# A two-layer hybrid encoder trunk: ScalarE's order in the first phase, and six modulation pieces of each mixer loaded into idle activation slots

## The chip, the core and the metric

The kernel runs on one core of one Trainium2 chip. A core has a matrix engine (TensorE, PE in the profile; its weight loads are listed apart as PEld), a vector engine (VectorE, DVE), an activation engine (ScalarE, ACT), a general engine (GpSimd, POOL) and a sequencer that here issues all data transfers (SyncE, SP). Each engine works through its own list of instructions in order and waits on semaphores for the others. Sixteen DMA engines move data between the chip's memory (HBM) and the core's memory (SBUF); matrix products land in a small accumulator memory (PSUM).

The metric is device microseconds of one execution. The time before is the median of three runs.

## The reference

One input of 256 tokens by 1024 channels goes through two layers. Each layer is a mixer and a squared-ReLU MLP, each with a norm ahead of it and behind it, and each modulated by shift, scale and gate vectors that come from a conditioning vector `c`:

```python
def hybrid_layer(x, c, ada_w, ada_b, ...):
    mod = jax.nn.silu(c) @ ada_w + ada_b
    sh_m, sc_m, gt_m, sh_f, sc_f, gt_f = [t[:, None, :] for t in jnp.split(mod, 6, axis=-1)]
    h = rms_norm(x, g_pre_mix) * (1.0 + sc_m) + sh_m
    proj = h @ w_in                      # rq rk rv rg lx ly fq fk fv ff gates
    ...                                  # retention, RG-LRU recurrence, forgetting attention
    merged = g[:, :, 0] * (y_ret @ ret_w_o) + g[:, :, 1] * (y_lru @ lru_w_o) + g[:, :, 2] * (y_fox @ fox_w_o)
    x = x + gt_m * rms_norm(merged @ w_out, g_post_mix)
    h = rms_norm(x, g_pre_mlp) * (1.0 + sc_f) + sh_f
    f = jnp.square(jax.nn.relu(h @ w1)) @ w2
    return x + gt_f * rms_norm(f, g_post_mlp)
```

`mod` has 6 x 1024 values a layer; its weights `ada_w` are 1024 x 6144 float32 a layer. All weights are float32 and each is read once.

## The kernel before, in words

**Products.** Every float32 operand is split into a rounded part (`hi`) and the remainder (`lo`), and a product is three matmuls, hi by hi, hi by lo and lo by hi (`mm3`, lines 368 to 371). A weight piece of 1024 x 256 is 1 MB; it arrives as two transfers of 512 KB (`raw_half`, line 216) into a ring of five half buffers (`wraw`, `NRAW = 5`). ScalarE writes `hi` (line 240), VectorE writes `lo` (line 241) into one of four half-piece slots `wpair`, or into a slot named in `SLOTS`. The VectorE subtraction is the last reader of the ring buffer. One piece feeds one gemm of 48 matmuls with 256 columns. `prefetch` (line 309) keeps two or three pieces split ahead of the gemm that runs.

**Modulation.** `silu(c) @ ada_w` isn't done on TensorE: a piece of 256 columns, transposed, also comes as two halves into the same ring, and VectorE multiplies each half with the broadcast row `sir` and sums along the row (`ada_sum`, line 301; `ada_step`, line 303). These pieces are woven between the gemm pieces by `weight_order` (line 94): all of them are numbered in one list `ORDER`, and `pos` walks through it. `MIXR` says between which gemms of a mixer the pieces stand, counted from the mixer's end. Mixer 0 has 53 gemms and 12 pieces (`gt_m`, `sc_f`, `sh_f`, four each) behind its gemms 31 to 43; mixer 1 has 61 gemms and 8 pieces (`sc_f`, `sh_f`) behind its gemms 41 to 51. The last 28 gemms of both mixers are the same: fq0, w_l0 to w_l3, fv0 to fv3, fq1 to fq3, fk0 to fk3, g2 0 to 3, w_f 0 to 3, w_o 0 to 3. Counted from the first of them (gemm 25 in mixer 0, 33 in mixer 1) they are called place 0 to 27 below; the pieces stand at places 6 to 18 in mixer 0 and 8 to 18 in mixer 1.

**First phase** (`first_rows`, line 462). The first pieces come by rows of the contraction, so that work starts early: for each k of 0 to 7 a row piece of `sc_m` and `sh_m` weights (two halves) and a row piece of rv and rq/rk weights (two halves). x is turned and scaled by matmuls with a diagonal (`turned`, line 475) into four PSUM tiles of two k each; the first is read in place, the others are copied by ScalarE into `xr` (lines 534 to 536). For each k: VectorE sums the two modulation halves (`row_sums`), ScalarE makes the shift and the scale from them (`sums`, lines 507 and 508), then h (`hh`, line 531, and its exact twin `hf`, line 532); VectorE writes `hl` (line 538); the two weight halves are split; TensorE runs 12 matmuls of 512 columns for rv and 24 of 256 columns for rq and rk (`rvp`, `qkp`). `qkp` needs the four PSUM tiles that held the turned x.

**Order.** A scheduler lays the instructions of each engine in a list at build time, by estimated ready times, with the program's order as the priority. `tc.keep_in_program_order` pins one instruction behind the one traced just before it on its engine.

**Activation slots.** `T1` to `T10` are large SBUF slots, reused in turn by tag (`U`, line 432). In a mixer `T5` holds the retention output until the `rg` gemms are through, `T6` the recurrent branch's `u` until the gelu gate of `ly3` (line 929), `T7` and `T8` its two helpers until the recurrence is through. From fk0 (place 12) on `T5` and `T6` hold the keys and `T7` and `T8` the attention's output. `prefetch` reaches two gemms ahead.

Of the kernel before, what the change touches and what calls it, by code (L numbers as in the profile page):

```python
# [16 lines left out]
KH = 4  # L17
# [16 lines left out]
P = 128  # L34
# [35 lines left out]
def mix_order(l):  # L70
    first = 'g0 g0 g0 g0 lx lx g1 lx g1 lx lru' if l == 0 else \
            'rv rv rv rv rq rk g0 rq rk g0 lx g0 lx g0 lx g1 lx lru g1'
    rest = 'rg rg rg rg g1 w_r w_r w_r w_r g1 ly ly ly ly fq w_l w_l w_l w_l fv fv fv fv fq fq fq fk fk fk fk ' \
           'g2 g2 g2 g2 w_f w_f w_f w_f w_o w_o w_o w_o'
    order = first.split() + rest.split()
    return [(n, order[:i].count(n)) for i, n in enumerate(order)]
# [10 lines left out]
    return name in ('rv', 'w_o', 'w2') or (name == 'w1' and cix < 4)  # L87


MIXR = ((22, 8), (20, 8))  # L90
MLPR = ((5, 28), (5, 15))


def weight_order():
    order = [(n, 0, k) for k in range(KD) for n in ('ada_row', 'row')]

    def spread(l, gem, ada, lo, hi):
        at = [lo + (hi - lo) * i // max(len(ada), 1) for i in range(len(ada))]
        for i, (n, c) in enumerate(gem):
            order.append(('gemm', l, n, c))  # L100
            while at and at[0] <= i:
                at.pop(0)
                order.append(ada.pop(0))
        assert not ada

    for l in range(L):
        n = len(mix_order(l))
        parts = [(l, p) for p in ('gt_m', 'sc_f', 'sh_f')][l:]
        spread(l, mix_order(l), [('ada',) + p + (c,) for p in parts for c in range(4)], *(n - i for i in MIXR[l]))
        parts = [(l, 'gt_f')] + [(i, p) for i in range(l + 1, L) for p in ('sc_m', 'sh_m', 'gt_m')]  # L110
        spread(l, mlp_order(), [('ada',) + p + (c,) for p in parts for c in range(4)], *MLPR[l])
    return order
# [6 lines left out]
def trunk_kernel(ctx, tc, x, c, vec, con, ffw, wts, out):  # L119
# [91 lines left out]
    def raw_half(i, extra=None):  # L211
        n = C if extra is None else C + NH_F
        t = wp.tile([P, KH, n], F32, name="wraw", tag="wraw", bufs=NRAW)
        src = wts[pos[0], i]
        if extra is None:
            nc.sync.dma_start(t.rearrange("p k c -> p (k c)"), src)
        else:
            nc.sync.dma_start(t[:, :, :C], src.rearrange("p (k c) -> p k c", k=KH))
            nc.sync.dma_start(t[:, :, C:], extra[:, i * KH:(i + 1) * KH, :])
        return t  # L220
# [25 lines left out]
    def load_split(l, name, cix):  # L246
        with ExitStack() as stack:
            if (name, cix) in LATE:
                for i in behind.pop(l, ()):
                    stack.enter_context(tc.issue_after(i))  # L250
            return split_of(l, name, cix)
# [44 lines left out]
    def mod_bias(l, o, n, src):  # L296
        V.tensor_tensor(mods[l][:, o:o + n], src, vc(l, 'ada_b')[:, o:o + n], ALU.add)

    def ada_sum(t, m):
        t = t.rearrange("p k c -> p (k c)")  # L300
        V.scalar_tensor_tensor(t, t, 0.5, sir, ALU.mult, ALU.mult, accum_out=m)  # L301

    def ada_step(l, part, cix):
        m = sp.tile([P, 2], F32, name="mcol")
        for j in range(2):
            ada_sum(raw_half(j), m[:, j:j + 1])
        pos[0] += 1
        mod_bias(l, PARTS[part] * 8 + 2 * cix, 2, m)

    ahead = []  # L310

    def prefetch(n=2):
        while len(ahead) < n and pos[0] < len(ORDER):
            o = ORDER[pos[0]]
            if o[0] == 'gemm':
                ahead.append((o[1:], load_split(*o[1:])))
            else:
                ada_step(*o[1:])

# [140 lines left out]
    def first_rows():  # L460
# [13 lines left out]
        def turned(k0):  # L474

            pt = pa.tile([P, 2, 2, P], F32, name="xT", tag="a")
            for k in range(2):
                for t in range(2):
                    T.matmul(pt[:, k, t, :], xs[:, t, (k0 + k) * P:(k0 + k + 1) * P], diag[:, t, :],
                             start=k == t == 0, stop=k == t == 1, skip_group_check=True)  # L480
            return pt.rearrange("p k t c -> p k (t c)")
# [23 lines left out]
        def sums(k, m):  # L505
            kc, o = slice(k, k + 1), 8 * PARTS['sh_m'] + k
            A.activation(a[:, kc], m[:, 0:1], AF.Identity, bias=one[:, kc], scale=vc(0, 'pre_mix')[:, kc])
            A.activation(sh[:, kc], m[:, 1:2], AF.Identity, bias=vc(0, 'ada_b')[:, o:o + 1])

        def halves(k, j, copy=A.copy):  # L510
# [12 lines left out]
        xT = [turned(0)]  # L523
        rv = [[pool.tile([P, 2, C], F32, name="rvp", tag=tag) for pool, tag in ((pg, "g"), (pz, "z"))]
              for t in range(2)]
        for k in range(KD):
            load(2 * k + FIRST_AHEAD + 2)
            kc, f = slice(k, k + 1), tmp("t1", "hf")[:, 0, :]
            wh, wl = halves(k, 0, A.copy if k else V.tensor_copy)
            xk = xr[:, k, :] if k else xT[0][:, 0, :]  # L530
            A.activation(hh[:, k, :], xk, AF.Identity, bias=sh[:, kc], scale=a[:, kc])
            A.activation(f, xk, AF.Identity, bias=sh[:, kc], scale=a[:, kc])
            if k == 0:
                A.copy(xr[:, 1, :], xT[0][:, 1, :])
                for k0 in (2, 4, 6):
                    A.copy(xr[:, k0:k0 + 2, :], turned(k0))
                qk = [[pa.tile([P, 2, S], F32, name="qkp", tag="a") for i in range(2)] for j in range(2)]
            V.tensor_tensor(hl[:, k, :], f, hh[:, k, :].bitcast(F32), ALU.subtract)
            for j in range(2):
                for t in range(2):  # L540
                    tk = slice(t * P, (t + 1) * P)
                    mm3(rv[t][j].rearrange("p h c -> p (h c)"), hh[:, k, tk], hl[:, k, tk], wh[:, j, :], wl[:, j, :],
                        k == 0, k == KD - 1)
            if k + 1 < KD:
                sums(k + 1, row_sums(k + 1))
            wh, wl = halves(k, 1)
            if k == KD - 1:
                nc.sync.dma_start(csb[:, P:5 * P], con[:, P:5 * P])
                early.extend(raw_half(j) for j in range(2))
                nc.sync.dma_start(csb[:, 5 * P:], con[:, 5 * P:])  # L550
            for j in range(2):
                for i in range(2):
                    for m in range(2):
                        n, cs = 2 * j + i, slice(m * P, (m + 1) * P)
                        mm3(qk[j][i][:, m, :], wh[:, n, cs], wl[:, n, cs], hh[:, k, :], hl[:, k, :], k == 0 and m == 0,
                            k == KD - 1 and m == 1, skip_group_check=True)
# [128 lines left out]
              'w_l': 1.7, 'fq': 2.4, 'fv': 2.4, 'fk': 2.4, 'g2': 3.0, 'w_f': 1.2, 'w_o': 1.0}  # L685

    def mixer(l, nm, h=None, rvp=None, qkp=None):
        hh, hl = h or nm.h

        def G(name, i, x=None, natural=False):  # L690
# [552 lines left out]
```

## Time and profile before

| | |
|---|---|
| median of 3 runs | 1122.72 us (1122.46 to 1124.48) |
| the profiled execution | 1122.77 us, span of the profile 1121.0 us |
| granted TensorE clock | 0.999 |
| read from HBM | 253 MB, 227 GB/s over the span |

The profile's page lists busy time by engine, the costliest groups of instructions, and a chain that is followed back from the last instruction. Further views group instructions in chosen stretches of time (windows), show one engine's instructions in order of time (timeline; in brackets the idle time before an instruction and what ended it) and who waited for whom (waits: total us, times, longest). PE counts as busy while a modelled matmul is in flight, so the lost time of a stretch is better taken from two stretches with the same work than from idle time alone.

### The profile page before, as it was taken

The numbers are of one execution on the slowest core, as the hardware profiler recorded it, in microseconds if no ns is written. First come the engines' busy times: TensorE is split into PE (matmuls) and PEld (weight loads), VectorE is DVE, ScalarE is ACT, GpSimd is POOL, SyncE is SP. The second block draws the span as 40 slices with busy tenths as digits, with TensorE's granted clock in tenths as the row PEclk, the third lists the DMA queues.
The fourth block names the chain that finished last, engine by engine and source line by source line (L and its number), as shares of the span: only waits on it lengthen the run. The fifth ranks groups of instructions, "written<-read, shape, count | busy, mean of one in ns | idle before, by whom it ended". The sixth has DMA issues, their size and how long they took to land.

```text
span 1121.0 us, 20568 instructions
## 1 busy us (share of the span) xinstructions
PE 1099.2 (98%) x8208; PEld 1037.1 (93%) x8208; DVE 870.5 (78%) x1324; ACT 617.4 (55%) x924; POOL 47.0 (4%) x62
## 2 busy tenths in 40 slices
PE   8999999999999999999999999999999999999997
PEld 7999999998899889989879999999999997989986
DVE  5998788878797789888487768887878778866543
ACT  5686595644355546445455657755445655544441
POOL 1001000000000110000030010000000003000000
PEclk9999999999999999999999999999999999999999
DMA  9954646678886569998735455566678584886541
GB/s 364 407 181 158 195 137 214 194 248 294 286 266 222 188 213 335 338 333 306 278 136 188 139 185 186 164 213 198 235 267 284 184 283 134 281 276 195 197 156 59
DMA packets 74284, 255.43 MB, mean 228 GB/s; under 512 B 10108, under 2 KB 12492, under 8 KB 74188
## 3 DMA queue, kind: packets, MB, share of 16 engines
q1 hardware_dynamic: 74188, 254.12, 66.5%
q8 instruction: 64, 1.05, 0.4%
q14 instruction: 32, 0.26, 0.1%
HBM read 253.00 MB, written 1.09 MB: 227 GB/s over the span
## 4 chain that ended last, share of the span: by engine, by line
PE 73%; DVE 9%; DMA 8%; issue 4%; ACT 3%; POOL 1%; SPq 0%; DVEq 0%; POOLq 0%; ACTq 0%
PE ps L371 22%; PE ps L369 21%; PE ps L370 21%; DMA wraw<-in_wts_dram 8%; DVE wpair L241 3%; DVE wraw L301 2%; ACT wpair L240 1%; POOL rs_v L198 1%; ACT junk L450 1%; POOL rs_r L199 1%; PE rvp L369 1%; PE rvp L370 0%; PE qkp L370 0%; PE qkp L371 0%; PE qkp L369 0%
## 5 line engine op out<-in xcount | busy, mean ns | idle before, releaser
L241 DVE TENSOR_TENSOR wpair<-wraw,wpair 128x1024 fp32r<-128x1024 f32 (+1 forms) x286 | 347.4, 1220 | 76.6 <-ACT wpair L240 74.7
L240 ACT CAST wpair<-wraw 128x1024 fp32r<-128x1024 f32 (+1 forms) x286 | 298.5, 1049 | 192.6 <-PE ps L371 128.7
L369 PE MATMUL ps<-hh,wpair 128*128 128x256 f32 x1312 | 364.4, 278 | 3.6 <-DVE fvl L701 2.6
L371 PE MATMUL ps<-hh,wpair 128*128 128x256 f32 x1312 | 362.9, 277 | 0.1
L370 PE MATMUL ps<-hl,wpair 128*128 128x256 f32 x1312 | 362.7, 276 | 0.0
L369 PEld LDWEIGHTS ps<-hh,wpair 128*128 128x128 f32 x1312 | 246.4, 188 | 4.7 <-DVE fvl L701 3.0
L371 PEld LDWEIGHTS ps<-hh,wpair 128*128 128x128 f32 x1312 | 246.3, 188 | 0.3 <-DVE wpair L241 0.3
L370 PEld LDWEIGHTS ps<-hl,wpair 128*128 128x128 f32 x1312 | 246.3, 188 | 0.2
L301 DVE SCALAR_TENSOR_TENSOR wraw<-wraw,sir 128x1024 f32<-128x1024 f32 x82 | 100.0, 1221 | 40.2 <-DMA wraw<-in_wts_dram 40.0
L241 DVE TENSOR_TENSOR wown<-wraw,wown 128x1024 fp32r<-128x1024 f32 x72 | 87.5, 1221 | 26.7 <-ACT wown L240 26.3
L240 ACT CAST wown<-wraw 128x1024 fp32r<-128x1024 f32 x72 | 74.8, 1048 | 55.9 <-DMA wraw<-in_wts_dram 30.3
L369 PE MATMUL ps<-wpair,mih 128*128 128x512 f32 x144 | 56.3, 391 | 0.0
L370 PE MATMUL ps<-wpair,mih 128*128 128x512 f32 x144 | 56.1, 389 | 0.0
L371 PE MATMUL ps<-wpair,mil 128*128 128x512 f32 x144 | 56.0, 389 | 0.0
L369 PE MATMUL ps<-wpair,hh 128*128 128x256 f32 (+1 forms) x144 | 45.6, 317 | 0.0
L370 PE MATMUL ps<-wpair,hh 128*128 128x256 f32 (+1 forms) x144 | 45.4, 316 | 0.0
L371 PE MATMUL ps<-wpair,hl 128*128 128x256 f32 (+1 forms) x144 | 45.4, 315 | 0.0
L369 PE MATMUL ps<-hh,wown 128*128 128x256 f32 x160 | 44.2, 276 | 0.0
L371 PE MATMUL ps<-hh,wown 128*128 128x256 f32 x160 | 44.2, 276 | 0.0
L370 PE MATMUL ps<-hl,wown 128*128 128x256 f32 x160 | 44.2, 276 | 0.0
L369 PE MATMUL ps<-wown,mih 128*128 128x512 f32 x112 | 43.7, 390 | 0.0
L370 PE MATMUL ps<-wown,mih 128*128 128x512 f32 x112 | 43.6, 389 | 0.0
(348 smaller groups left out, 2303.3 us busy)
## 6 DMA issues: line engine op xcount, KB each, us to landing
wraw<-in_wts_dram SPq DMA_DIRECT2D x440, 512.0 KB, 4.3
wfirst<-in_wts_dram SPq DMA_DIRECT2D x28, 512.0 KB, 10.2
rows<-drow SPq DMA_DIRECT2D x10, 512.0 KB, 6.1
xs<-in_x_dram SPq DMA_DIRECT2D x2, 512.0 KB
out_dram<-xs SPq DMA_DIRECT2D x4, 256.0 KB, 2.0
csb<-in_con_dram SPq DMA_DIRECT2D x1, 768.0 KB
csb<-in_con_dram SPq DMA_DIRECT2D x1, 256.0 KB, 9.6
vsb<-in_vec_dram SPq DMA_DIRECT2D x1, 152.0 KB, 6.5
```

Of the source, the lines that this page charges most:

```text
L198: pin(nc.gpsimd.tensor_scalar(v, part, rest, None, ALU.add))
L199: nc.gpsimd.tensor_tensor(r, v, mhalf[:, :1], ALU.pow)
L240: copy(hi, t)
L241: V.tensor_tensor(lo, t, hi.bitcast(F32), ALU.subtract)
L301: V.scalar_tensor_tensor(t, t, 0.5, sir, ALU.mult, ALU.mult, accum_out=m)
L369: T.matmul(ps, ah, bh, start=start, stop=False, **kw)
L370: T.matmul(ps, ah, bl, start=False, stop=False, **kw)
L371: T.matmul(ps, al, bh, start=False, stop=stop, **kw)
L450: return A.activation(j, x, AF.Square, scale=D ** -0.5, accum_out=acc)
```

## The change

Three edits. In `first_rows`, the copy of the second k of x is pinned behind `hf` of k = 0, the other three copies are made (and pinned) only after ScalarE's cast of the second weight half of k = 0, and the shift and scale of k = 1 are made after them; VectorE's row sums of k = 1 are traced ahead of that cast as before. In `weight_order`, the modulation pieces of a mixer begin at place 0, and its first six are parked: their loads stand at places 0, 1, 2, 3, 7 and 9, go to the slots `T5`, `T6`, `T7`, `T8`, `T5`, `T6` and not to the ring, and their sums are traced when the gemms at places 2, 4, 5, 7, 9 and 11 have been split, pinned in VectorE's list. The remaining pieces of mixer 0 (six) stand at places 10, 11, 13, 15, 16 and 18, those of mixer 1 (two) at 15 and 17.

```diff
-MIXR = ((22, 8), (20, 8))
+MIXR = ((28, 8), (28, 8))
+PARK = ('T5', 'T6', 'T7', 'T8')
+PARK_FROM = 28
+PARK_AT = (0, 1, 2, 3, 7, 9)
+PARK_DUE = (2, 4, 5, 7, 9, 11)
...
-    def spread(l, gem, ada, lo, hi):
+    def spread(l, gem, ada, lo, hi, parked=0):
         at = [lo + (hi - lo) * i // max(len(ada), 1) for i in range(len(ada))]
+        if parked:
+            first = len(gem) - PARK_FROM
+            at[:parked] = [first + d for d in PARK_AT[:parked]]
+            ada[:parked] = [a + (PARK[i % 4], first + PARK_DUE[i]) for i, a in enumerate(ada[:parked])]
...
-        spread(l, mix_order(l), [('ada',) + p + (c,) for p in parts for c in range(4)], *(n - i for i in MIXR[l]))
+        spread(l, mix_order(l), [('ada',) + p + (c,) for p in parts for c in range(4)], *(n - i for i in MIXR[l]),
+               parked=6)
...
-    def ada_step(l, part, cix):
-        m = sp.tile([P, 2], F32, name="mcol")
-        for j in range(2):
-            ada_sum(raw_half(j), m[:, j:j + 1])
+    parked = []
+
+    def ada_step(l, part, cix, home=None, due=None):
+        if home:
+            t = U(home, [P, 2, KH, C], F32, "wada")
+            for j in range(2):
+                nc.sync.dma_start(t[:, j].rearrange("p k c -> p (k c)"), wts[pos[0], j])
+            raws = [t[:, j] for j in range(2)]
+        else:
+            raws = [raw_half(j) for j in range(2)]
         pos[0] += 1
-        mod_bias(l, PARTS[part] * 8 + 2 * cix, 2, m)
+
+        def sums():
+            m = sp.tile([P, 2], F32, name="mcol")
+            for j in range(2):
+                i = ada_sum(raws[j], m[:, j:j + 1])
+                if home:
+                    tc.keep_in_program_order(i)
+            mod_bias(l, PARTS[part] * 8 + 2 * cix, 2, m)
+
+        if home:
+            parked.append((due, sums))
+        else:
+            sums()
...
                 ahead.append((o[1:], load_split(*o[1:])))
+                gems[0] += 1
+                while parked and gems[0] > parked[0][0]:
+                    parked.pop(0)[1]()
...
+        pin = tc.keep_in_program_order
         for k in range(KD):
...
             if k == 0:
-                A.copy(xr[:, 1, :], xT[0][:, 1, :])
-                for k0 in (2, 4, 6):
-                    A.copy(xr[:, k0:k0 + 2, :], turned(k0))
-                qk = [[pa.tile([P, 2, S], F32, name="qkp", tag="a") for i in range(2)] for j in range(2)]
+                pin(A.copy(xr[:, 1, :], xT[0][:, 1, :]))
+                xT += [turned(k0) for k0 in (2, 4, 6)]
...
             if k + 1 < KD:
-                sums(k + 1, row_sums(k + 1))
+                m = row_sums(k + 1)
+                if k:
+                    sums(k + 1, m)
             wh, wl = halves(k, 1)
+            if k == 0:
+                for i in (1, 2, 3):
+                    pin(A.copy(xr[:, 2 * i:2 * i + 2, :], xT[i]))
+                sums(1, m)
+                qk = [[pa.tile([P, 2, S], F32, name="qkp", tag="a") for i in range(2)] for j in range(2)]
...
     def mixer(l, nm, h=None, rvp=None, qkp=None):
+        gems[0] = len(ahead)
```

More of the change, by code (lines that the diff above doesn't have):

```diff
@@ L300, in ada_sum @@
         t = t.rearrange("p k c -> p (k c)")
-        V.scalar_tensor_tensor(t, t, 0.5, sir, ALU.mult, ALU.mult, accum_out=m)
-    def ada_step(l, part, cix):
-        m = sp.tile([P, 2], F32, name="mcol")
-        for j in range(2):
-            ada_sum(raw_half(j), m[:, j:j + 1])
-        pos[0] += 1
-        mod_bias(l, PARTS[part] * 8 + 2 * cix, 2, m)
+        return V.scalar_tensor_tensor(t, t, 0.5, sir, ALU.mult, ALU.mult, accum_out=m)
+    parked = []
[7 more added lines that the diff above has]
+            raws = [raw_half(j) for j in range(2)]
+        pos[0] += 1
+        def sums():
[9 more added lines that the diff above has]
+            sums()
     ahead = []
+    gems = [0]
     def prefetch(n=2):
```

## Prediction

> **What bounds the kernel now.** The page comes first, for the span and the engines; then the windows view, to find the stretches where TensorE waits; then the timelines of those stretches.
>
> ```profile
> span 1121.0 us, 20568 instructions
> ...
> PE 1099.2 (98%) x8208; PEld 1037.1 (93%) x8208; DVE 870.5 (78%) x1324; ACT 617.4 (55%) x924; POOL 47.0 (4%) x62
> ```
>
> TensorE is busy for 1099.2 of 1121.0 us, so 21.8 us of idle time is about all that a change of order can reach. The profiled execution took 1122.77 us, 1.77 more than its span and 0.05 from the median 1122.72; every sum below is made against it.
>
> ```profile
> core 0: us, PE busy (x) PEld busy (x) DVE busy (x) ACT busy (x) POOL busy (x), PEclk, DMA share, GB/s
> ...
> 30.00:40.00 10.00, 10.00 (x70) 9.18 (x69) 9.29 (x13) 7.07 (x12) 0.00 (x0) 1.00 1.03 410
> 14.20:27.69 13.49, 11.81 (x73) 10.20 (x73) 9.87 (x14) 7.82 (x15) 0.00 (x0) 1.00 1.03 409
> 213.93:354.29 140.36, 133.71 (x1143) 131.61 (x1143) 113.42 (x228) 66.16 (x111) 0.00 (x0) 1.00 0.77 255
> 767.37:899.59 132.22, 131.97 (x1142) 131.17 (x1142) 104.52 (x205) 65.94 (x110) 0.00 (x0) 1.00 0.71 239
> 200.00:230.00 30.00, 30.00 (x267) 30.00 (x267) 24.30 (x29) 17.27 (x23) 0.00 (x0) 1.00 0.62 194
> 230.00:320.00 90.00, 83.53 (x709) 81.85 (x708) 74.04 (x146) 36.49 (x56) 0.00 (x0) 1.00 0.84 284
> ```
>
> ```profile
> 213.93 0.69 DVE L929 TENSOR_TENSOR ge<-ge,lru_u 128x512 f32<-128x512 f32 x1
> ...
> 354.29 0.68 DVE L1078 SCALAR_TENSOR_TENSOR ml<-gate,mh 128x512 fp32r<-128x512 f32 x1
> ...
> 767.37 0.69 DVE L929 TENSOR_TENSOR ge<-ge,lru_u 128x512 f32<-128x512 f32 x1
> ...
> 899.59 0.68 DVE L1078 SCALAR_TENSOR_TENSOR ml<-gate,mh 128x512 fp32r<-128x512 f32 x1
> ```
>
> Two stretches matter. The third and fourth window run from the last gelu gate with `u` (L929) to the first `ml` (L1078) in mixer 0 and in mixer 1: the same gemms, 1143 and 1142 matmul records, but **140.36 against 132.22 us**. Mixer 0 has twelve modulation pieces there and mixer 1 eight. The 8.14 us is lost TensorE time, and the waits view of the two says how:
>
> ```profile
> PE ps L369 <- DVE fvl L701: 2.6, 2, 1.4
> PE ft L997 <- DVE sm L991: 1.9, 2, 1.1
> PE fs L370 <- DVE fkl L701: 0.8, 1, 0.8
> ```
>
> The same view of VectorE's waits, mixer 0 and then mixer 1:
>
> ```profile
> DVE wraw L301 <- DMA wraw<-in_wts_dram: 14.6, 13, 2.5
> ...
> DVE wraw L301 <- DMA wraw<-in_wts_dram: 9.9, 7, 2.6
> ```
>
> TensorE waits for VectorE's small results (`fvl`, `sm`, `fkl`). They are late because VectorE, which works in order, stands before a modulation sum whose half hasn't landed: 14.6 us in 13 waits in mixer 0, and 9.9 us in 7 waits in mixer 1, where TensorE has no wait long enough to be listed. The halves are late because a ring buffer must come free before the next is issued: the ring moves 284 GB/s at a DMA share of 0.84 in 230 to 320 us, while 30 us earlier only 194 GB/s is asked for and 410 GB/s is reached where many loads are out at once.
>
> The other stretch is the first phase:
>
> ```profile
> 10.51 3.39 PE L479 MATMUL xT<-diag,xs 128*128 128x128 f32 x28 [1.29 <-ACT diag L472]
> 14.20 1.20 PE L369 MATMUL rvp<-wpair,hh 128*128 128x512 f32 x4 [0.30 <-ACT hh L531]
> 21.66 1.21 PE L369 MATMUL rvp<-wpair,hh 128*128 128x512 f32 x4 [1.40 <-ACT hh L531]
> 27.69 0.74 PE L369 MATMUL rvp<-wpair,hh 128*128 128x512 f32 x2 [0.23 <-ACT hh L531]
> ...
> 33.42 0.47 PE rvp L369 x2
> ...
> 55.32 0.47 PE rvp L369 x2
> ```
>
> From k = 3 (33.42) to k = 7 (55.32; these two are from the chain of work) a step takes 21.90 / 4 = 5.475 us. The first two took 7.46 and 6.03 us: 13.49 − 10.95 = **2.54 us lost**, besides 0.30 ahead of k = 0. All three waits are for ScalarE's `hh`.
>
> **The change part by part: the first phase.** ScalarE and VectorE there:
>
> ```profile
> 12.15 0.58 ACT L536 COPY xr<-xT 128x512 f32<-128x512 f32 x1 [1.69 <-PE xT L479]
> 12.63 0.30 ACT L508 ACTIVATE mod<-mrow,vsb 128x1 f32<-128x1 f32 x1
> ...
> 13.10 0.57 ACT L536 COPY xr<-xT 128x512 f32<-128x512 f32 x1
> 13.57 0.57 ACT L531 ACTIVATE hh<-xT,mod 128x256 fp32r<-128x256 f32 x1
> ...
> 15.21 1.09 ACT L240 CAST wpair<-wfirst 128x1024 fp32r<-128x1024 f32 x1
> ...
> 10.76 0.16 DVE L520 SCALAR_TENSOR_TENSOR one_sc<-vsb 128x8 f32<-128x8 f32 x1
> 11.28 0.70 DVE L240 CAST wpair<-wfirst 128x1024 fp32r<-128x1024 f32 x1 [0.36 <-DMA wfirst<-in_wts_dram]
> ...
> 16.33 1.22 DVE L241 TENSOR_TENSOR wpair<-wfirst,wpair 128x1024 fp32r<-128x1024 f32 x1 [1.27 <-ACT wpair L240]
> 17.47 1.22 DVE L301 SCALAR_TENSOR_TENSOR wfirst<-wfirst,sir 128x1024 f32<-128x1024 f32 x1
> ```
>
> No instruction is added or removed; ScalarE's order moves. (a) Two copies of x (12.15 and 13.10) stand ahead of `hh`, and the shift and scale waited behind the first, though VectorE had their inputs at 10.92. The first tile of the turned x, a quarter of the transposes, is there by about 11.1 if the tiles are filled in order. Without the copies: shift and scale 10.95 to 11.5, `hh` to 12.0, `hf` to 12.5, the pinned copy to 12.75. TensorE is then held by its own 28 transposes, whose last starts about 13.6; k = 0 starts at 13.75, **0.45 earlier**. (b) The cast at 15.21 stood behind all the copies. It now follows at 12.75, since its half lands about 1.3 us (512 KB at 410 GB/s) after the one that VectorE cast at 11.28. VectorE's `lo` of it moves from 16.33 to 13.7, the sums of k = 1 from 17.47 to about 14.9 (that half and the two that are summed land 1.3 us apart after 11.28, by 15.1), and end at 17.3. Then `hh` of k = 1 is done at 18.2, before TensorE ends k = 0 at 13.75 + 5.475 = 19.2: the 1.40 us wait goes. (c) What is late next is VectorE: `lo` and `hl` of k = 1, two sums and two `lo`, at the 1.14 us from 16.33 to 17.47 each, and two `hl` at about 0.4: 5 x 1.14 + 0.8, 6.5 us from 17.3, end at 23.8; TensorE wants k = 2 at 24.7. So k = 2 starts at 24.7 in place of 27.69, 3.0 us earlier, with 0.9 to spare. The margin is less than one such instruction, so I take **2.7**; the bounds are 0.5 ((a) alone) and 3.0. The copies that move back are hidden: `qkp` needs their PSUM at 13.75 + 2.7 = 16.5, and they end at 15.2. If the cast got in front of `hh`, its 1.09 would put `hh` at about 14.1, and the start 0.4 later. What follows keeps the gain, since VectorE moves 3 us ahead too.
>
> The loads must follow: a step needs four halves, 2.10 MB, 5.11 us at the 410 GB/s of the row 30 to 40, less than 5.475. The Trainium skill, "DMA: Bandwidth & Descriptors", Specifications, speaks against this: about 358 GB/s for one core from HBM. By that a step's rows would take an estimated 5.9 us and the first phase would gain nothing. The trace disagrees, with 410 GB/s over 10 us.
>
> **The parked pieces.** A parked piece is two loads, two sums of 1.22 us and a small add, as before; only their places and slots change. Six pieces of mixer 0 leave the ring; at places 10 to 18 stand six instead of eight (places 6 to 9 had the other four). Mixer 1 also has six there now, and two at 8 and 9, and its TensorE loses 132.22 − 131.97 = 0.25 us. VectorE's work stays 113.4 us; in 133 us that is 85%, below the 93% that it holds from 30 to 40 us, where TensorE doesn't wait. So the most that mixer 0 can give is 8.14, the least 0. I take **6.6**: near mixer 1's row, with 1.5 left since four more sums, 9.8 us, stay in VectorE's list and half of the `sm` and `ptl` waits lie where pieces remain. Mixer 1 has 0.25 to give at most; I take 0.1.
>
> Where the loads go: places 0 to 3 get four pieces in some 22 us, 4.2 MB or 190 GB/s, on the 194 GB/s of 200 to 230 us. The sum, 385, is below the 410 seen. A parked piece ahead of a weight half delays it by 2 x 1.3 us.
>
> ```profile
> 199.40 0.33 SPq L216 DMA_DIRECT2D wraw<-in_wts_dram  x1
> ...
> 213.16 1.06 ACT L240 CAST wpair<-wraw 128x1024 fp32r<-128x1024 f32 x1 [0.59 <-PE ps L371]
> 221.32 0.69 DVE L898 SCALAR_TENSOR_TENSOR mt<-gate,ps 128x512 f32<-128x512 f32 x1 [0.36 <-PE ps L371]
> ...
> 320.50 24.90 SPq L216 DMA_DIRECT2D wraw<-in_wts_dram  x10
> 345.45 0.43 SPq L576 DMA_DIRECT2D drow<-rrow  x1
> ...
> wraw<-in_wts_dram SPq DMA_DIRECT2D x440, 512.0 KB, 4.3
> ```
>
> One new wait is plain: place 1's load into `T6` needs the end of the last read of `u` (L929 at 213.93), 214.6, and the program puts it behind w_l0's second half, issued at 199.40. Queued behind it on SP are w_l1's halves, whose cast ran at 213.16 for a gemm that starts at 221.3. Held to 214.6 they would land about 222 (two parked and two own halves at 1.3 us, from 215, and latency), and with cast and `lo`, 2.3 us, TensorE would wait 3 us, once a mixer. Against it: the program traces `drow`'s transfer at w_f0, ahead of the loads of w_f1 to w_f3, yet it was issued at 345.45, straight behind a run of ten ring loads (row 320.50): the scheduler lets loads pass one that isn't ready. I take 0, bounds 0 and 6. POOL has no work in either window.
>
> Sum: 2.7 + 6.6 + 0.1 = 9.4; 1122.7 − 9.4 = **1113.3 us**.
>
> **The rivals.**
> *Only one part works.* Parking gives little: the stalls move to the pieces still in the ring, as `sm` at 1.9 us hints; against it stands mixer 1's row. 2.7 and up to 2: 1118 to 1120. Or the first phase gives 0.5: rows land too late, or VectorE's list keeps sums behind `lo`; then 1122.7 − 0.5 − 6.7 = 1115.5. The Trainium skill's 358 GB/s would end here too; with 410 in the trace it has a fiftieth.
> *It doesn't do what it says.* The scheduler's lists put the parked loads behind ring loads, so they land no earlier, and the copies' pins change nothing: within 2 us of 1122.7.
> *Slower: a parked sum reaches VectorE before its load.* SP is in order too. Where a parked load is listed behind a weight half that waits for a ring buffer which VectorE frees just before that sum, VectorE waits the full 4.3 us from issue to landing (last row above) where 2.6 was free in mixer 1: 1.7 to 4.3 us a piece, 3 in the middle. Pieces with only two gemms between load and sum (places 0, 7 and 9, three a mixer, six in all) would lose 18 us; less 2.7 that is 1138. It decides from four such pieces (12 us against 9.4). Against it: two gemms are 10.9 us.
>
> **How the numbers follow.** Both parts 0.61, about 1113.3 (1110.8 to 1116); parking alone 0.12, 1115.5; first phase alone 0.13, 1119; no effect 0.07, 1122; slower 0.07, 1138. Two tenths of a per cent, 2.2 us, is about what a measurement of this kernel can tell from no change. The forecast is that of the first case, 0.61. A fifth of the first-phase case falls within it: faster 0.83, same 0.10, slower 0.07. The range runs from all of 3.0 + 8.14 + 0.25 and a little more, 1110.8, to the first phase alone, 1120.0.
>
> **What would show it.** Right: rvp of k = 1 and 2 start near 19.2 and 24.7 without a wait; the stretch from L929 to L1078 in mixer 0 takes 133 to 135 us; DVE's wait for `wraw` there falls from 14.6 to under 9. Wrong: DVE waits for a parked load (`wada`), SP waits long at a parked load's line while casts wait for DMA, or mixer 1's stretch is above 133.

## The result, and the profile after

The kernel after takes 1111.67 us (median of three executions, 1111.37 to 1112.15) where the kernel before took 1122.72: a ratio of 0.9889 [0.9868, 0.9910], 11.05 us less. In a later measurement it was 1112.36 against 1122.40, 0.9910 [0.9896, 0.9925], 10.04 us less. The profiled execution took 1112.15 us.

The page of the kernel after: the span, the busy times by engine, the modulation sums that are left in the ring (count, busy us, mean ns; idle time ahead of them and what ended it) and the loads of the parked pieces (count, size, median us to landing).

```profile
span 1110.4 us, 20558 instructions
...
PE 1096.9 (99%) x8208; PEld 1037.0 (93%) x8208; DVE 871.7 (79%) x1324; ACT 618.1 (56%) x924; POOL 46.0 (4%) x62
...
L310 DVE SCALAR_TENSOR_TENSOR wraw<-wraw,sir 128x1024 f32<-128x1024 f32 x58 | 70.7, 1222 | 25.3 <-DMA wraw<-in_wts_dram 25.1
...
wada<-in_wts_dram SPq DMA_DIRECT2D x24, 512.0 KB, 5.9
```

The same group on the page of before:

```profile
L301 DVE SCALAR_TENSOR_TENSOR wraw<-wraw,sir 128x1024 f32<-128x1024 f32 x82 | 100.0, 1221 | 40.2 <-DMA wraw<-in_wts_dram 40.0
```

The work of each engine is the same to within 2.3 us. Twenty-four sums, the six parked pieces of both mixers at two halves each, have left the ring, and VectorE's idle time ahead of the sums in the ring fell from 40.2 to 25.3 us.

Where the time went is read from the windows view, with the span cut into five: up to the first gelu gate of mixer 0, from there to its first `ml`, the MLP and what lies around it, the same stretch of mixer 1, and the rest. This stretch of a mixer begins three gelu gates earlier than that of the prediction, since in some runs below the last gate itself moved. Before, then after:

```profile
0.00:197.55 197.55, 191.25 (x1541) 184.62 (x1541) 165.33 (x264) 133.61 (x219) 10.04 (x15) 1.00 0.67 236
197.55:354.29 156.74, 150.09 (x1288) 147.99 (x1287) 128.24 (x246) 77.50 (x126) 0.00 (x0) 1.00 0.75 249
354.29:750.99 396.70, 395.25 (x2795) 366.61 (x2795) 316.00 (x433) 225.38 (x319) 25.56 (x29) 1.00 0.68 231
750.99:899.59 148.60, 148.35 (x1287) 147.55 (x1286) 119.34 (x223) 77.28 (x125) 0.00 (x0) 1.00 0.70 234
899.59:1121.00 221.41, 214.24 (x1307) 190.34 (x1305) 141.56 (x163) 103.65 (x137) 11.35 (x18) 0.99 0.58 196
```

```profile
0.00:195.19 195.19, 191.29 (x1540) 185.14 (x1541) 165.36 (x263) 133.99 (x219) 9.23 (x15) 1.00 0.71 253
195.19:344.05 148.86, 148.12 (x1287) 147.45 (x1286) 128.65 (x245) 77.80 (x126) 0.00 (x0) 1.00 0.72 241
344.05:740.91 396.86, 395.42 (x2796) 366.66 (x2796) 315.51 (x433) 225.08 (x319) 25.44 (x29) 1.00 0.70 239
740.91:888.89 147.98, 147.81 (x1287) 147.33 (x1286) 120.48 (x223) 77.54 (x125) 0.00 (x0) 1.00 0.66 216
888.89:1110.40 221.51, 214.27 (x1307) 190.38 (x1306) 141.73 (x163) 103.68 (x137) 11.38 (x18) 1.00 0.58 195
```

The gains are 2.36, 7.88, −0.16, 0.62 and −0.10 us; their sum is the 10.6 by which the span shrank. In the prediction's narrower stretches mixer 0 went from 140.36 to 132.48 us and mixer 1 from 132.22 to 131.61. All of it lies in the first stretch and in the two mixers. The waits view of mixer 0 from the last gelu gate to the first `ml` (211.57 to 344.05) has these of VectorE for the ring's sums and of TensorE for VectorE:

```profile
DVE wraw L310 <- DMA wraw<-in_wts_dram: 5.7, 4, 3.3
...
PE fo L400 <- DVE ptl L739: 0.6, 1, 0.6
```

Before it was 14.6 us in 13 waits, and TensorE's waits for `fvl`, `sm` and `fkl`. Those three are gone, one of 0.6 us for `ptl` is left, and VectorE waits for no parked load: `wada` is not in the view as something that VectorE waited for.

The first phase of after, in the timelines of TensorE, ScalarE and VectorE (in brackets the idle time ahead and what ended it):

```profile
12.72 1.17 PE L400 MATMUL rvp<-wpair,hh 128*128 128x512 f32 x4
...
19.24 1.20 PE L400 MATMUL rvp<-wpair,hh 128*128 128x512 f32 x4 [0.77 <-ACT hh L563]
...
25.27 0.73 PE L400 MATMUL rvp<-wpair,hh 128*128 128x512 f32 x2 [0.24 <-ACT hh L563]
```

```profile
17.45 0.29 ACT L539 ACTIVATE mod<-mrow,vsb 128x1 f32<-128x1 f32 x1 [0.76 <-DVE wfirst L310]
17.66 1.03 ACT L249 CAST wpair<-wfirst 128x1024 fp32r<-128x1024 f32 x1
18.59 0.59 ACT L563 ACTIVATE hh<-xr,mod 128x256 fp32r<-128x256 f32 x1
```

```profile
15.05 1.22 DVE L310 SCALAR_TENSOR_TENSOR wfirst<-wfirst,sir 128x1024 f32<-128x1024 f32 x1
...
18.72 1.23 DVE L250 TENSOR_TENSOR wpair<-wfirst,wpair 128x1024 fp32r<-128x1024 f32 x1 [1.30 <-ACT wpair L249]
```

The sums of k = 1 start at 15.05 as forecast (14.9), but a step later ScalarE's list has something that the prediction did not: behind the shift of k = 1 (L539) stands the cast of that k's rv weights, and only then `hh`. The cast stood at that place before the change too (its lines are below). The shift waits for the second sum, the cast waits behind it for nothing, VectorE stands idle for 1.30 us, and TensorE waits 0.77 us for `hh`.

### The profile page after: what moved, and what is told of

It is laid out like the page before. It is cut to its first block, busy times and chain, and to the rows that moved or that the text cites. A ratio compares the mean times of both kernels' runs of the same rounds, so it can differ in the third digit from the quotient of the medians.

```text
span 1110.4 us, 20558 instructions
## 1 busy us (share of the span) xinstructions
PE 1096.9 (99%) x8208; PEld 1037.0 (93%) x8208; DVE 871.7 (79%) x1324; ACT 618.1 (56%) x924; POOL 46.0 (4%) x62
## 4 chain that ended last, share of the span: by engine, by line
PE 83%; DVE 7%; ACT 3%; DMA 3%; issue 2%; POOL 2%; SPq 0%; DVEq 0%; POOLq 0%; ACTq 0%
PE ps L402 25%; PE ps L401 25%; PE ps L400 25%; DMA wraw<-in_wts_dram 2%; DVE wpair L250 2%; ACT wpair L249 1%; POOL rs_v L207 1%; POOL rs_r L208 1%; DVE xs L662 1%; PE rvp L400 1%; PE rvp L401 0%; PE qkp L401 0%; PE qkp L400 0%; PE qkp L402 0%; PE rvp L402 0%
## 5 line engine op out<-in xcount | busy, mean ns | idle before, releaser
L310 DVE SCALAR_TENSOR_TENSOR wraw<-wraw,sir 128x1024 f32<-128x1024 f32 x58 | 70.7, 1222 | 25.3 <-DMA wraw<-in_wts_dram 25.1
```

Source lines behind the costliest of these rows:

```text
L310: return V.scalar_tensor_tensor(t, t, 0.5, sir, ALU.mult, ALU.mult, accum_out=m)
```

## The experiments

The theory behind the prediction has two parts: ScalarE's order in the first phase is worth 2.7 us, and in mixer 0 modulation halves held ring buffers that weight halves needed, so that pieces taken out of the ring free 6.6. The rivals tested: only one part works; spreading the pieces over more places did it, and not the slots; the parked sums are near to reaching VectorE before their loads. All runs were timed against the kernel before on the same chip, in three sets. The first phase alone, the parked pieces alone, the new places in the ring and the first run with the cast moved have a median before of 1122.31; the slots at the old places, the sums sooner, the second run with the cast moved and the kernel after again have 1122.40; the last four runs have 1122.62.

**The first phase alone.** All pieces in the ring at their old places, `first_rows` as after:

```diff
-MIXR = ((28, 8), (28, 8))
+MIXR = ((22, 8), (20, 8))
...
-               parked=6)
+               parked=0)
```

> The first-phase edit alone; the modulation pieces of the mixers stand and load as before the change. Theory A (two independent parts; the first phase gives what the two profiles differ by at the last gelu gate of mixer 0, 213.93 to 211.57, 2.4 us): 1120.3 us, rvp of k = 2 at about 25.3 us, mixer 0's stretch from the last gelu gate with u to the first ml still 140.4 us, SP's waits for the ring as before. Theory B (part of those 2.4 us is GpSimd's second pow, 1.38 us in the profile of before and 0.57 in that of after, which no edit touches): the median gains only 1.5 to 1.9 us, 1121.0 us.

1122.19 us, ratio 1.000 [0.9987, 1.0012]: no gain that can be measured, so both numbers missed. Yet its first gelu gate comes at 195.38, 2.17 us earlier than before. The windows view of the two mixers shows where this profile gave it back:

```profile
195.38:349.94 154.56, 149.76 (x1287) 147.85 (x1286) 128.20 (x245) 77.29 (x126) 0.00 (x0) 1.00 0.74 251
349.94:746.72 396.78, 395.36 (x2796) 366.72 (x2796) 315.43 (x433) 224.87 (x319) 25.66 (x29) 1.00 0.68 232
746.72:899.09 152.37, 149.36 (x1287) 147.84 (x1286) 119.21 (x224) 77.51 (x125) 0.00 (x0) 1.00 0.68 228
```

Mixer 1 took 152.37 where it had taken 148.60, though its lists of instructions on VectorE, GpSimd and SyncE are those of before. Either the edit reaches it in some way, or this stretch takes another time in each execution. Two runs of the last set were made to tell that apart.

**The parked pieces alone.** `first_rows` as before, all else as after:

```diff
-                pin(A.copy(xr[:, 1, :], xT[0][:, 1, :]))
-                xT += [turned(k0) for k0 in (2, 4, 6)]
+                A.copy(xr[:, 1, :], xT[0][:, 1, :])
+                for k0 in (2, 4, 6):
+                    A.copy(xr[:, k0:k0 + 2, :], turned(k0))
...
-                m = row_sums(k + 1)
-                if k:
-                    sums(k + 1, m)
+                sums(k + 1, row_sums(k + 1))
...
```

> The parking edit alone; the first phase is that of before. Theory A (independent parts): mixer 0's stretch 132.5 us in place of 140.4, mixer 1's 131.6 in place of 132.2, together 8.5 us: 1114.2 us, and the gains of the two parts alone add to the 11.05 us of both. Rival: the parts lean on each other (a first phase that ends earlier leaves the loads further ahead), then parking alone gives under 7 us, above 1115.7 us.

1113.92 us, ratio 0.9926 [0.9906, 0.9945], as the first theory had it. Its mixers take 149.71 and 147.97 us. So the parked pieces carry most of the gain, 8.4 of 10 to 11 us. The timeline of TensorE in its first phase, which has the old order, is of use below:

```profile
13.06 1.20 PE L400 MATMUL rvp<-wpair,hh 128*128 128x512 f32 x4 [0.30 <-ACT hh L563]
...
26.56 0.74 PE L400 MATMUL rvp<-wpair,hh 128*128 128x512 f32 x2 [0.23 <-ACT hh L563]
```

**New places, but in the ring.** The six pieces of each mixer are loaded at the new places 0, 1, 2, 3, 7 and 9, into ring buffers, and summed there:

```diff
-            ada[:parked] = [a + (PARK[i % 4], first + PARK_DUE[i]) for i, a in enumerate(ada[:parked])]
```

> The kernel after, but the six pieces stand at their new places 0, 1, 2, 3, 7 and 9 in the ring of five half buffers, with their sums traced right behind their loads; no activation slot is used. Theory slots (what limits is the ring: a modulation half holds a ring buffer from its issue to its sum): mixer 0's stretch keeps at least half of its 8 us, 136 us or more, VectorE waits over 10 us for wraw there, and mixer 1 gains nothing; 1115 to 1119 us. Theory places (what limits is how densely the pieces stand, twelve pieces over 13 gemms; spread over 19 gemms the ring suffices): mixer 0's stretch 132.5 to 133.5 us, 1111.7 to 1112.7 us.

1116.62 us, ratio 0.9950 [0.9931, 0.9969], between the two. The windows of the two mixers and VectorE's wait in mixer 0:

```profile
195.53:347.80 152.27, 148.94 (x1288) 147.84 (x1287) 127.74 (x246) 77.56 (x126) 0.00 (x0) 1.00 0.76 256
745.15:893.10 147.95, 147.78 (x1287) 147.30 (x1286) 120.00 (x223) 77.49 (x125) 0.00 (x0) 1.00 0.69 234
```

```profile
DVE wraw L309 <- DMA wraw<-in_wts_dram: 15.0, 9, 4.1
```

In mixer 1, which has eight pieces, wider places are enough: 147.95 us with no slot in use. In mixer 0, which has twelve, they leave 15.0 us of VectorE's waits and 152.27 us.

**Slots, at the old places.** The counterpart: mixer 0 keeps the order of before, and the pieces at its places 6 to 11 go to `T5` to `T8`; mixer 1 isn't parked.

```diff
-MIXR = ((28, 8), (28, 8))
+MIXR = ((22, 8), (20, 8))
...
-PARK_AT = (0, 1, 2, 3, 7, 9)
-PARK_DUE = (2, 4, 5, 7, 9, 11)
+PARK_AT = (6, 7, 8, 9, 10, 11)
+PARK_DUE = (8, 9, 10, 11, 11, 11)
...
-               parked=6)
+               parked=0 if l else 6)
```

> Only mixer 0's pieces change: the six pieces at the places 6 to 11, in the old order, go to T5 to T8 and not to the ring; the other six keep their old places in the ring, mixer 1 and the first phase are those of before. Theory slots (what was short is ring buffers: a sum that is late holds a buffer that a weight half needs): the stretch from the first gelu gate to the first ml of mixer 0, 156.74 us before and 148.86 after, takes 151 or less and the whole about 1115. Theory places (what was short is VectorE's room and the DMA's between places 6 and 18, where twelve pieces stand close): little changes, 155 to 157 and about 1121. Both needed, as the run with new places in the ring (152.26) makes likely: 152 to 153.5, the whole near 1118.

1113.39 us, ratio 0.9920 [0.9905, 0.9935]. The expectation says that the first phase is that of before; in the kernel it is that of after, so this run differs from the first phase alone by the six pieces of mixer 0 and nothing else: they have slots, and their sums are pinned in VectorE's list up to two gemms behind their loads. The windows of its mixers, and VectorE's wait in mixer 0:

```profile
195.17:343.29 148.12, 147.80 (x1287) 147.32 (x1286) 129.05 (x246) 77.53 (x126) 0.00 (x0) 1.00 0.72 244
740.08:889.30 149.22, 148.69 (x1287) 147.62 (x1286) 119.66 (x224) 77.33 (x125) 0.00 (x0) 1.00 0.69 231
```

```profile
DVE wraw L310 <- DMA wraw<-in_wts_dram: 0.3, 1, 0.3
```

This settles what was short in mixer 0. The loads' places are those of before, the bytes and VectorE's work (129.05 us, 128.24 before) are nearly the same, and the stretch takes 148.12 us with 0.3 us of waits. Neither the transfers' rate nor VectorE's room was the limit, but the ring's buffers. SyncE's waits for a buffer that a modulation sum still held show it directly; here from 195 to 354 us, before and then in this run:

```profile
SPq L216 <- DVE wraw L301: 30.9, 19, 3.8
```

```profile
SPq L225 <- DVE wraw L310: 6.9, 8, 1.2
```

ScalarE's waits for weight halves fell with them, from 24.5 to 7.3 us. The theory of the slots is right, its 151 not even low enough, and "both needed" is wrong. That the sums also stand later is not what does it, to judge by the next run, which has them early again. A ring of more buffers with all else as before, which would be the plainest test, was not run.

**Sums sooner.** The kernel after with each parked sum traced at the gemm whose prefetch loads it, or one later:

```diff
-PARK_DUE = (2, 4, 5, 7, 9, 11)
+PARK_DUE = (0, 1, 2, 3, 7, 9)
```

> The kernel after with each parked sum traced at the gemm whose prefetch loads it or one later (places 0, 1, 2, 3, 7, 9 in place of 2, 4, 5, 7, 9, 11). Theory distance (the rival of the prediction, a sum that reaches VectorE before its load, is real and only the distance of two or more gemms avoids it): VectorE waits for wada, at least 2 us a mixer at the piece in T6, whose load can't start before u has been read; mixer 0 from first gelu gate to first ml 151 or more, the whole 1114 to 1118. Rival: the pieces' own slots are enough, since no weight half needs them: VectorE waits but TensorE has two gemms split ahead, mixer 0 within 0.5 of 148.9 and the whole about 1112.

1112.82 us, ratio 0.9918 [0.9903, 0.9933]. The first parked sum of mixer 0 starts at 211.24 where the kernel after has it at 216.4, and the waits view has no wait of VectorE for `wada`. What it has in mixer 0 (149.51 us) are waits of the ring's sums, and one of TensorE:

```profile
DVE wraw L310 <- DMA wraw<-in_wts_dram: 6.8, 4, 3.3
...
PE fo L400 <- DVE ptl L739: 1.2, 1, 1.2
```

Each of the six sums of mixer 0 starts 5 to 14 us earlier than in the kernel after and none waits, so they have at least 5 us in hand there, and the slower rival was not near. The expectation's own rival had mixer 0 within 0.5 of 148.9; 149.51 is just outside.

**The cast behind the shift, taken away.** The kernel after, with the shift of k = 1 pinned behind the cast of that k's rv weights, run twice:

```diff
-            wh, wl = halves(k, 0, A.copy if k else V.tensor_copy)
+            wh, wl = nxt if k == 1 else halves(k, 0, A.copy if k else V.tensor_copy)
...
-                sums(1, m)
+                kn = slice(1, 2)
+                A.activation(a[:, kn], m[:, 0:1], AF.Identity, bias=one[:, kn], scale=vc(0, 'pre_mix')[:, kn])
+                nxt = halves(1, 0)
+                o = 8 * PARTS['sh_m'] + 1
+                pin(A.activation(sh[:, kn], m[:, 1:2], AF.Identity, bias=vc(0, 'ada_b')[:, o:o + 1]))
```

> The kernel after, with the shift of k = 1 pinned behind ScalarE's cast of the rv weights of k = 1 (before, the cast came behind the shift and in front of hh). Theory C (after the change the first phase is bounded by the chain through VectorE and ScalarE: VectorE stood idle for 1.30 us ahead of the lo of k = 1, because the cast waited behind the shift): that lo starts at about 17.8 in place of 18.72 us, rvp of k = 1 at 18.6 or before and of k = 2 at 24.4 in place of 25.27: 0.9 us less, 1110.8 us. Rival: the sums of k = 2 wait for their rows' loads or for lo of the other half all the same, and k = 2 starts at 25.0 or later: within 0.3 us of 1111.7.

> The kernel with the shift of k = 1 pinned behind the cast of the rv weights of k = 1, beside the kernel after on the same chip: theory of the sum (0.66 us earlier at k = 2 is kept to the end): 0.4 to 0.9 us less than the kernel after. Rival (an MLP 0 that is bound otherwise takes it back, as the first profile of it showed, 205.93 for 203.76): no difference, within 0.3 us.

1111.88 us, ratio 0.9909 [0.9887, 0.9930], and 1112.09, ratio 0.9909 [0.9892, 0.9927]; the kernel after in the second set had 1112.36. k = 2 starts at 24.61 and 24.81 without a wait, as the cause says, and the first gelu gate comes 0.6 to 0.8 us earlier than after. That much the times of so few executions can't tell. In the first of the two runs the MLP's stretch took 397.98 us and ate the gain; in the second it took 396.79, so that loss does not belong to the edit. The second lost time in mixer 0 instead:

```profile
194.40:342.69 148.29, 148.11 (x1287) 147.43 (x1286) 128.78 (x246) 77.36 (x126) 0.00 (x0) 1.00 0.73 243
```

```profile
194.61:344.39 149.78, 148.09 (x1287) 147.42 (x1286) 128.66 (x245) 77.76 (x126) 0.00 (x0) 1.00 0.72 241
```

**The kernel after, again.**

> The kernel after, unchanged, a second profile and twelve or more further times beside the others: 1111.7, its first phase with the second GpSimd power at 0.57 us, mixer 0 from first gelu gate to first ml within 0.6 of 148.86 and mixer 1 within 0.3 of 147.99. If those stretches differ by a microsecond or more, differences of that size between the other runs mean nothing.

1112.36 us (1111.74 to 1113.39). Its mixers in the windows view:

```profile
195.27:344.12 148.85, 148.12 (x1287) 147.45 (x1286) 128.62 (x246) 77.58 (x126) 0.00 (x0) 1.00 0.73 242
...
740.92:888.88 147.96, 147.79 (x1287) 147.31 (x1286) 120.45 (x223) 77.59 (x125) 0.00 (x0) 1.00 0.65 215
```

Both stretches are within 0.02 us of the first profile. For mixer 0 that is partly luck: VectorE has the same list there in the run of the parked pieces alone and in the two with the cast moved, and those took 149.71, 148.29 and 149.78 us. They differ in TensorE's wait for VectorE's `ptl`, which is 1.4 us, not listed, and 1.5 us; in both profiles of the kernel after it is 0.6.

**The kernel before and the first phase alone, again.**

> The kernel before, unchanged. Theory variation (a stretch in which every half waits for a ring buffer takes another time in each execution, with the same lists): its second profile shows mixer 0 from first gelu gate to first ml anywhere in 154 to 158 and mixer 1 in 148.5 to 153, off the first profile's 156.74 and 148.61 by 0.5 or more in at least one, and its times lie over 3 us or more. Theory lists (times follow the lists of instructions): both stretches within 0.3 of the first profile, as in the two profiles of the kernel after, and the 3.8 us that mixer 1 lost in the run of the first phase alone came from its edit.

> The first phase alone, a second time. Theory kept (the 2.2 us by which its first gelu gate came earlier stay on the mean, and the first measurement, 1.000 [0.9987, 1.0012], hid them behind the variation of the mixers): mixer 1 near 149 in this profile and a mean of 1.5 to 2 us below the kernel before. Theory lost (what the first phase gives without the parked pieces is given back in the mixers, on the mean): mixer 1 again near 152 and a mean within 0.7 us of the kernel before.

The kernel before: 1122.09 us (1120.96 to 1124.64). The first phase alone: 1121.34 us (1118.05 to 1124.16), ratio 0.9993 [0.9982, 1.0003]. The mixers of the first:

```profile
197.65:352.87 155.22, 149.92 (x1287) 147.84 (x1286) 128.34 (x246) 77.26 (x126) 0.00 (x0) 1.00 0.75 250
...
749.59:898.58 148.99, 148.51 (x1287) 147.66 (x1286) 119.42 (x223) 77.18 (x125) 0.00 (x0) 1.00 0.69 234
```

and of the second:

```profile
195.02:348.43 153.41, 149.51 (x1287) 147.72 (x1286) 128.39 (x246) 77.30 (x126) 0.00 (x0) 1.00 0.75 254
...
745.55:895.00 149.45, 148.58 (x1287) 147.55 (x1286) 119.57 (x223) 77.05 (x125) 0.00 (x0) 1.00 0.69 233
```

The same program gave 156.74 and 155.22 in mixer 0, the other 154.56 and 153.41, and in mixer 1 152.37 and 149.45. So the stretch does vary with the same program: at least 2.9 of the 3.8 us that mixer 1 lost in the first run of the first phase alone do not come from its edit. The means: 24 executions of the first phase alone 1121.65, 40 of the kernel before in the same two sets 1122.35, a difference of 0.70 with an interval of ± 0.79. The theory "kept" expected 1.5 to 2 and "lost" less than 0.7. Neither is clearly met.

**The old places with all else of after,** and the same with the pinned cast. The first is the run with slots at the old places, with mixer 1 as after:

```diff
-MIXR = ((22, 8), (20, 8))
-PARK_AT = (6, 7, 8, 9, 10, 11)
-PARK_DUE = (8, 9, 10, 11, 11, 11)
+MIXR = ((22, 8), (28, 8))
+PARK_AT = ((6, 7, 8, 9, 10, 11), (0, 1, 2, 3, 7, 9))
+PARK_DUE = ((8, 9, 10, 11, 11, 11), (2, 4, 5, 7, 9, 11))
...
-               parked=0 if l else 6)
+               parked=6)
```

> All of the kernel after but for mixer 0, where the twelve pieces stand at the old places (6 to 11 and 13 to 18) and the first six go to T5 to T8. With the first phase of after and mixer 1 of after. Against the run with the old places in mixer 0 and mixer 1 as before it, this tells what mixer 1's pieces are worth: theory of the profile (mixer 1's 149.22 becomes 147.96): 1112.1, 1.3 less. Theory nothing (mixer 1 lost little in the prediction's row): 1113.2. Against the kernel after it tells whether places matter at all once the slots are there: mixer 0 from first gelu gate to first ml 148.1 for 148.86, so 0.7 below after at best, 1111.6.

> The run before this one with the shift of k = 1 pinned behind the cast of the rv weights of k = 1. If each gain in a profile is kept to the end: k = 2 at 24.7, 0.6 us less than that run, about 1111.2 and below the kernel after by about 1. Rival: no difference that the times can tell, as in the two runs of that edit on the kernel after.

1111.76 us (1111.39 to 1112.26), ratio 0.9908 [0.9895, 0.9921], and 1111.10 us (1110.23 to 1112.13), ratio 0.9904 [0.9889, 0.9918]. The windows of the mixers of the second run:

```profile
194.28:342.25 147.97, 147.80 (x1287) 147.32 (x1286) 128.94 (x245) 77.75 (x126) 0.00 (x0) 1.00 0.71 245
739.53:887.48 147.95, 147.78 (x1287) 147.30 (x1286) 120.60 (x223) 77.52 (x125) 0.00 (x0) 1.00 0.64 215
```

In both runs both mixers stand at 147.95 to 147.97 us, although mixer 0 has four more pieces: no cost of those four is to be seen. Its span, 1108.8 us, is the shortest of all profiles, 1.6 less than after's, but the intervals of the ratios overlap with that of the kernel after, so a better kernel is likely and not shown. Mixer 1's new order, the only difference between the two runs with the old places and the cast unmoved, is 1.63 us by the medians, which are of two sets, and 1.26 by the two profiles (149.22 to 147.96), as the theory of the profile had it. It need not be the slots: the new places in the ring gave mixer 1 the same 147.95.

## Why the prediction was right or wrong

The direction, the range (1110.8 to 1120.0) and the mechanism in mixer 0 held; the sum, 9.4 us, was 1.6 too small against the first measurement and 0.6 against the second. Two steps failed. The one that failed most is mixer 1's term, put at 0.1 with a ceiling of 0.25, where the profiles show 0.6 to 4.4. The other is `hh` of k = 1 in the first phase, forecast in time and late by about 1 us, so that this term was too large. The two errors have opposite signs, so that the sum came out near is in part luck. By its steps:

**(a) k = 0 at 13.75.** It started at 12.72. What the prediction did not know is GpSimd's second power, ahead of the turning of x: 1.38 us in the profile of before, 0.57 in that of after. Where it took the longer time with the new order, as in the second profile of the first phase alone, k = 0 started at 13.58. So the step is right, and about 1 us of what the two profiles differ there is not the edit's.

**(b) and (c) k = 1 at 19.2 without a wait, k = 2 at 24.7 with VectorE next.** The sums and the copies went as forecast. `hh` of k = 1 did not: it was forecast to be done at 18.2, before TensorE ends k = 0 at 19.2, and is done about 19.2 (18.59 + 0.59), since a cast of 1.03 us stands in front of it. The prediction had seen that danger for k = 0 and did not look for it at k = 1, where the profile of before already has it. Its ScalarE and VectorE:

```profile
20.07 1.03 ACT L240 CAST wpair<-wfirst 128x1024 fp32r<-128x1024 f32 x1
21.01 0.60 ACT L531 ACTIVATE hh<-xr,mod 128x256 fp32r<-128x256 f32 x1
...
21.14 1.23 DVE L241 TENSOR_TENSOR wpair<-wfirst,wpair 128x1024 fp32r<-128x1024 f32 x1 [1.29 <-ACT wpair L240]
```

VectorE's 1.29 us of idle time behind the sums is missing in the prediction's count of 6.5 us, and it is still there after (1.30). TensorE had ended k = 0 earlier, so it waited 0.77 us. That k = 1 started at 19.24, as forecast, is luck: k = 0 came 1 us early and `hh` 1 us late. With the long power k = 1 starts at 19.18 to 19.36 without a wait (the second run of the first phase alone, the sums sooner, the slots at the old places). The step from k = 1 to k = 2 did not shorten at all, 6.03 us before and after, so k = 2 came at 25.27. That the cast is the cause was shown: with the cast moved, k = 2 starts at 24.61 and 24.81.

**The first phase's 2.7.** Between the two profiles the first gelu gate moved by 2.36 us. In the run of the parked pieces alone, with the old order and the power at 0.57 us, k = 2 starts at 26.56 and the gate comes at 196.51; so 1.04 of the 2.36 is the power, and the edit's part is 1.32. Where the power takes the longer time the edit is worth 197.55 − 195.02 = 2.53, because with the new order k = 2 no longer follows it (25.09 with the long power, 25.27 and 25.46 with the short). The term was mis-sized: 1.3 to 2.5, not 2.7. The whole kernel shows 0.70 ± 0.79 for it alone. What becomes of the rest there stays open; the mixers' own variation is larger than what is asked for. Beside the parked pieces it is 1113.92 − 1112.36 = 1.6 us, by medians of two sets whose intervals overlap.

**Mixer 0's 6.6.** The two profiles gave 7.88, but the same kernel before gave 155.22 in its second, so 6.37 there: the term was as good as such a stretch can be told from one profile. The mechanism, halves that hold ring buffers, is shown by the run with slots at the old places. What was argued wrongly is the part that would be left, 1.5 for the four more sums in VectorE's list: with slots at the old places nothing of it is to be seen. With the slots at the new places some is left: five profiles with the kernel after's list there have 148.29 to 149.78, 149.10 on the mean, and the three with slots at the old places 148.02. So the new places, which came with the slots, are no help in mixer 0 and cost about 1 us by the profiles; the times can't tell it (1112.36 against 1111.76, of two sets).

**Mixer 1's 0.1, at most 0.25.** This is the step that failed most. In mixer 1 too VectorE stood before the ring's sums, without a wait of TensorE long enough to be listed: VectorE's wait for the ring's sums there fell from 9.9 us (7 waits) to 1.4 (3), and SyncE's wait for a buffer that such a sum held from 23.5 to 4.8. With the new places in the ring they are 3.9 and 19.6, and the gain is whole, so VectorE's wait is the better sign; by which of its results TensorE was held back is not shown. Five profiles without parked or spread pieces in mixer 1 have 148.60, 148.99, 149.22, 149.45 and 152.37 us, the kernel after has 147.98 and 147.96: 0.6 to 4.4 us, 1.8 on the mean. The prediction took the ceiling from 132.22 − 131.97, the stretch less TensorE's busy time. Busy time counts a matmul that is in flight, so it holds lost time too: it fell itself, from 148.35 to 147.81 in the wider stretch. And it rested on one profile of a stretch that varies, which happened to be the fastest of the five.

With the means of the profiles in the place of those terms, 1.9 for the first phase (the middle of 1.3 and 2.5), 154.98 − 149.10 = 5.9 for mixer 0 (four profiles and five) and 1.8 for mixer 1, the sum is 9.6, near the 10.0 and 11.05 that were measured.

**The wait of place 1's load for `u`,** taken at 0 with a bound of 6, cost TensorE nothing. The timeline of SyncE's queue in the kernel after:

```profile
191.38 19.91 SPq L225 DMA_DIRECT2D wraw<-in_wts_dram  x8
212.34 0.80 SPq L318 DMA_DIRECT2D wada<-in_wts_dram  x2
213.43 0.33 SPq L225 DMA_DIRECT2D wraw<-in_wts_dram  x1
```

The last read of `u` starts at 211.57 and takes 0.69 us; the load is issued at 212.34, right behind it, and eight ring loads were listed ahead of it. SyncE stood 1.0 us for it, and TensorE has no listed wait from 195 to 230 us. The list lets the ring loads pass, as the prediction read from `drow`.

**The rivals.** "Only the first phase" is refuted by 1113.92 for the parked pieces alone, "does nothing" by the ratio, and the slower one by the run with sooner sums. That the first phase gives only 0.5 is not refuted by its own runs, but its part in the profiles, 1.3 to 2.5, speaks against it. The rule that would have ended the first phase's gain, the 358 GB/s of the Trainium skill, "DMA: Bandwidth & Descriptors", Specifications, does not bind on this core. The page of the kernel after has 409 GB/s in its second slice, 27.8 us long, and the step from k = 0 to k = 2 shortened:

```profile
GB/s 361 409 204 156 188 185 261 253 269 247 285 175 251 183 252 325 322 327 308 265 155 170 157 191 166 214 283 277 215 211 207 163 256 152 286 267 195 198 155 58
```

The Trainium skill says itself, on the same page under Bandwidth, Measured, that one core streaming alone goes above that share (425 GB/s in a 16 MB transfer), and with that the trace agrees.

## What to carry to other kernels

When a second stream shares a ring of buffers with the one that feeds TensorE, look for its waits in the engine that empties the ring, and first give the second stream buffers of its own; here that was worth 5 to 9 us in one mixer with no load at another place and no byte less, while spreading it over more places gave less than half of that there (2.7 of 7.0 us on the means of the profiles). In the other mixer, with fewer pieces, spreading was enough. A stretch can lose time to such a ring although the engine that is fed shows no wait worth listing. Don't take a stretch's time less its busy time for all that it can give, nor one profile of such a stretch for its time. And when an order of instructions is corrected at one step of a loop, read the same engine's list at the next step too: here a cast stood in front of `hh` at k = 1, before the change and after it, and not at k = 0.

## What the runs showed that was not expected

GpSimd's second power of 128 values takes 0.57 us in eight of the 14 profiles and 1.38 to 1.64 in the other six, in the same program too. The timelines of GpSimd in the two profiles of the first phase alone:

```profile
8.08 0.57 POOL L208 TENSOR_TENSOR rs_r<-rs_v,mhalf 128x1 f32<-128x1 f32 x1
```

```profile
8.31 1.63 POOL L208 TENSOR_TENSOR rs_r<-rs_v,mhalf 128x1 f32<-128x1 f32 x1
```

The order of before passes that on to all that follows (k = 2 at 27.69 and 27.71 with the long power, 26.56 with the short); the new order does not. What makes it take longer was not tried.

A stretch in which sums and weights wait for the same ring varies by microseconds from one execution to the next with the same lists: mixer 0 took 153.4 to 156.7 us in four profiles without slots, 148.29 to 149.78 in the five with slots at the new places, and 147.96 to 148.12 in the three with slots at the old places. The 65 timed executions of the kernel before lie between 1118.78 and 1126.12 us, the nine of the kernel after between 1111.37 and 1113.39; nine are too few to say that its times are steadier, and the six of the second run with the cast moved lie between 1110.88 and 1114.79.
